# Gate/up- and down-projection of a decoder layer as 2x2 block products with 7 multiplications

## Chip, cores and metric

The kernel runs on one core of one Trainium2 chip, in one launch. The metric is the time of the run on the device in microseconds (us), as the median of several runs; lower is better. All inputs lie in HBM, and the result is written to HBM.

## What is computed

One pre-norm decoder layer over 512 tokens and a model width of 2048, in float32. Three token mixers (the functions are left out here) give `mix`; it is projected and added to the residual, a second RMSNorm feeds a gated MLP with a causal convolution of width 3 over the tokens, and a last RMSNorm closes.

```python
D_MODEL, SEQ, D_FF, CONV_W = 2048, 512, 5632, 3

def rms_norm(x, g):
    x32 = x.astype(jnp.float32)
    y = x32 * lax.rsqrt(jnp.mean(x32 * x32, axis=-1, keepdims=True) + EPS)
    return (y * g.astype(jnp.float32)).astype(x.dtype)

def conv_glu_ffn(h, w_up, conv_w, conv_b, w_down):
    a = h @ w_up
    a = lax.conv_general_dilated(a, conv_w[:, None, :], window_strides=(1,),
                                 padding=[(CONV_W - 1, 0)], ...) + conv_b
    gate, up = a[..., :D_FF], a[..., D_FF:]
    return (jax.nn.silu(gate) * up) @ w_down

x = x + mix @ w_out[l]
h = rms_norm(x, norm_ffn[l])
x = x + conv_glu_ffn(h, w_up[l], conv_w[l], conv_b[l], w_down[l])
return rms_norm(x, norm_final)
```

## The kernel before

Everything is held transposed: model or hidden columns lie on the 128 partitions, the 512 tokens along the free axis. A weight block of 128 x 128 is the stationary operand of a matmul, an activation tile of 128 x 512 the moving one. Each float32 operand X is split in two, `hi` (ScalarE's copy to fp32r, line 81 for weights) and `lo` = X - `hi` (VectorE, line 82), and each block product is three matmuls into one PSUM bank: hi by hi, hi by lo, lo by hi (`step`, lines 95 to 97; `accumulate` runs it over the inner blocks). `split` (lines 106 and 107) does the same for activations.

Weights come in pieces of up to `WS` = 1024 columns, 8 blocks: `stage` (lines 74 to 83) loads one on SyncE's DMA queue into one of two `raw` buffers and splits it into one of four `hi` and one of four `lo` buffers, at high priority, so that loads and splits stand as early in each engine's row as the buffers allow. `tiles_of` cuts a weight row into two such pieces. The Tile framework sets the order of each engine's instructions and the waits between them.

The mixers fill the first 674 us. Then come:

- The out-projection (674 to 849 us): 16 rows `d` of 16 blocks. `resid(d, ps)` loads the residual `x` on GpSimd's queue (line 747), adds the result (748), scales and splits it into the normalization's numerator `hh` and `hl` (754, 755), squares it on ScalarE (761) and sums the squares on GpSimd into `sacc` (762). All 16 tiles of the new residual, `x2`, stay in SBUF.
- The FFN (from 849 us): `FG` = 4 groups of `FT` = 11 hidden tiles. `up(f)` is two units, gate and up, of 16 blocks and 48 matmuls of 512 columns each. The first call also forms the row scale `rs2` from `sacc`. `conv` (lines 783 to 786) scales each result by `rs2` out of PSUM, and adds the three taps on ScalarE and VectorE; then come SiLU, the gating product (798) and the split into `hidh`, `hidl`, which stay in SBUF. After 11 of these, the down-projection of the group: for each of 16 rows `d`, 11 blocks, 33 matmuls, and one VectorE addition onto `x2[d]`.
- The last group's down-projection: the first 7 blocks of each row as before; the last `NL` = 4 blocks in two halves of 256 tokens (`last`, lines 841 to 843, addition in 845). `finish(0)`, the final norm of the first half with its output, stands inside the second half; `finish(1)` (lines 860 to 871) ends the kernel: the row scale `r3s` and one scaling for each row, partly on VectorE (870).

## Time and profile before

| | |
|---|---|
| Time, median of 3 runs (lowest to highest) | 2304.11 us (2303.01 to 2304.51) |
| Span of the profiled execution (its own time) | 2303.2 us |
| TensorE busy | 2275.0 us, 99% |
| VectorE busy | 1217.3 us, 53% |
| ScalarE busy | 878.4 us, 38% |
| GpSimd busy | 87.0 us, 4% |
| DMA, mean over the span | 98 GB/s |

The profile is of one execution, and its own time is the span; that is 0.9 us under the median of the runs. PE is TensorE's matmul row, PEld its weight loads, which lie beside matmuls, DVE is VectorE, ACT ScalarE, POOL GpSimd and SP SyncE. A matmul's recorded duration is longer than its share of the engine, since matmuls overlap; how much of TensorE one takes is read from the distance between the starts of two. Busy time of an engine says how much it had to do, not whether anything waited for it; the chain that ended last and the idle time in front of instructions say that.

### The profile page before, as it was taken

How to read it: one execution, taken by the hardware profiler on the slowest of the kernel's cores; microseconds unless marked ns; L12 is line 12 of the kernel's file. 1: busy time of each engine (PE TensorE's matmuls, PEld its weight loads, DVE VectorE, ACT ScalarE, POOL GpSimd, SP SyncE). 2: the span in 40 equal slices, each digit the busy share in tenths (PEclk: the TensorE clock that was granted, in tenths of full speed). 3: DMA queues.
4: the chain of work that ended last, by engine and by line, in shares of the span. 5: the costliest groups of instructions: out<-in, count | busy, mean ns of one | idle time of the engine just before them, and what ended most of it. 6: DMA issues, size and time to landing. Idle time of an engine off the chain costs nothing.

```text
span 2303.2 us, 27199 instructions
## 1 busy us (share of the span) xinstructions
PE 2275.0 (99%) x10788; PEld 1917.5 (83%) x10788; DVE 1217.3 (53%) x1991; ACT 878.4 (38%) x1272; POOL 87.0 (4%) x150
## 2 busy tenths in 40 slices
PE   8999999999999999999999999999999999999998
PEld 7988889888888888888888888888888888888887
DVE  7689576667675335444334444334544433454446
ACT  6536566755564223333223333222333222333223
POOL 4010000000011110000000000000000000000001
PEclk9999999999999999999999999999999999999999
DMA  5333322222233322232333322333233233323233
GB/s 180 103 96 123 100 78 74 74 71 83 89 118 121 101 93 99 92 100 84 95 105 101 101 94 91 91 99 111 92 100 96 84 95 110 101 94 99 71 113 110
DMA packets 72816, 226.49 MB, mean 98 GB/s; under 512 B 9220, under 2 KB 11674, under 8 KB 72688
## 3 DMA queue, kind: packets, MB, share of 16 engines
q1 hardware_dynamic: 67824, 211.40, 28.9%
q0 software_dynamic: 4720, 13.35, 1.7%
q8 instruction: 84, 1.38, 0.3%
q14 instruction: 44, 0.36, 0.1%
q10 hardware_dynamic: 144, 0.01, 0.0%
HBM read 220.50 MB, written 6.18 MB: 98 GB/s over the span
## 4 chain that ended last, share of the span: by engine, by line
PE 94%; DVE 2%; ACT 2%; DMA 1%; issue 1%; POOL 0%; DVEq 0%; ACTq 0%; POOLq 0%
PE pj L95 24%; PE pj L96 24%; PE pj L97 24%; PE mx L95 3%; PE mx L97 3%; PE mx L96 3%; PE pmv L205 1%; PE pmv L207 1%; PE pmv L206 1%; PE pa L440 1%; ACT hi L81 1%; DMA x<-in_xT_dram 1%; PE psc L284 0%; PE ptr L638 0%; DVE lo L82 0%
## 5 line engine op out<-in xcount | busy, mean ns | idle before, releaser
L81 ACT ACTIVATE hi<-raw 128x1024 fp32r<-128x1024 f32 (+5 forms) x438 | 420.3, 960 | 996.5 <-PE pj L96 764.3
L82 DVE TENSOR_TENSOR lo<-raw,hi 128x1024 fp32r<-128x1024 f32 (+5 forms) x438 | 483.7, 1105 | 461.1 <-ACT hi L81 460.7
L95 PE MATMUL pj<-hh,hi 128*128 128x512 f32 x1408 | 547.8, 389 | 0.0
L97 PE MATMUL pj<-hh,lo 128*128 128x512 f32 x1408 | 547.8, 389 | 0.0
L96 PE MATMUL pj<-hh,hi 128*128 128x512 f32 x1320 | 513.5, 389 | 0.0
L95 PEld LDWEIGHTS pj<-hh,hi 128*128 128x128 f32 x1408 | 264.4, 188 | 54.9
L97 PEld LDWEIGHTS pj<-hh,lo 128*128 128x128 f32 x1408 | 264.4, 188 | 54.7
L96 PEld LDWEIGHTS pj<-hh,hi 128*128 128x128 f32 x1320 | 247.9, 188 | 51.3
L95 PE MATMUL pj<-xh,hi 128*128 128x512 f32 (+1 forms) x608 | 232.2, 382 | 0.9 <-ACT ia L250 0.9
L96 PE MATMUL pj<-xl,hi 128*128 128x512 f32 (+1 forms) x608 | 231.7, 381 | 0.0
L97 PE MATMUL pj<-xh,lo 128*128 128x512 f32 (+1 forms) x608 | 231.0, 380 | 0.0
L783 DVE TENSOR_TENSOR a<-pj,rs 128x512 f32<-128x512 f32 x88 | 60.8, 691 | 291.4 <-PE pj L97 289.4
L95 PEld LDWEIGHTS pj<-xh,hi 128*128 128x128 f32 x608 | 114.2, 188 | 19.2 <-ACT ia L250 1.1
L97 PEld LDWEIGHTS pj<-xh,lo 128*128 128x128 f32 x608 | 114.2, 188 | 18.0
L96 PEld LDWEIGHTS pj<-xl,hi 128*128 128x128 f32 x608 | 114.3, 188 | 17.8
L95 PE MATMUL pj<-hidh,hi 128*128 128x512 f32 x320 | 124.5, 389 | 0.0
L96 PE MATMUL pj<-hidl,hi 128*128 128x512 f32 x320 | 124.5, 389 | 0.0
L97 PE MATMUL pj<-hidh,lo 128*128 128x512 f32 x320 | 124.5, 389 | 0.0
L95 PE MATMUL mx<-hidh,hi 128*128 128x512 f32 x320 | 124.5, 389 | 0.0
L96 PE MATMUL mx<-hidl,hi 128*128 128x512 f32 x320 | 124.5, 389 | 0.0
L97 PE MATMUL mx<-hidh,lo 128*128 128x512 f32 x320 | 124.5, 389 | 0.0
L97 PE MATMUL pj<-mh,lo 128*128 128x512 f32 x256 | 99.9, 390 | 0.0
(339 smaller groups left out, 3014.0 us busy)
## 6 DMA issues: line engine op xcount, KB each, us to landing
raw<-in_wu_dram SPq DMA_DIRECT2D x176, 512.0 KB, 3.6
raw<-in_wst_dram SPq DMA_DIRECT2D x76, 512.0 KB, 3.6
raw<-in_wd_dram SPq DMA_DIRECT2D x48, 384.0 KB, 3.1
raw<-in_wo_dram SPq DMA_DIRECT2D x32, 512.0 KB, 3.6
raw<-in_wd_dram SPq DMA_DIRECT2D x48, 320.0 KB, 2.9
x<-in_xT_dram POOLq DMA_DIRECT2D x32, 256.0 KB, 5.7
raw<-in_wcv_dram SPq DMA_DIRECT2D x8, 512.0 KB, 3.7
raw<-in_wai_dram SPq DMA_DIRECT2D x8, 512.0 KB, 3.8
```

The lines of the kernel that those rows point to most:

```text
L81: ACT.activation(hi[:, :cols], raw[:, :cols], AF.Copy)
L82: DVE.tensor_tensor(lo[:, :cols], raw[:, :cols], hi[:, :cols], op=ALU.subtract)
L95: PE.matmul(ps, wh, ah[:, lo:], start=first, stop=False)
L96: PE.matmul(ps, wh, al[:, lo:], start=False, stop=False)
L97: PE.matmul(ps, wl, ah[:, lo:], start=False, stop=last)
L205: PE.matmul(ps[t], ah[:, ts], wh, start=(k == 0), stop=False)
L206: PE.matmul(ps[t], al[:, ts], wh, start=False, stop=False)
L207: PE.matmul(ps[t], ah[:, ts], wl, start=False, stop=(k == KT - 1))
L440: PE.matmul(pa[:, c * 192:(c + 1) * 192], x[:, cc * P:(cc + 1) * P], y[:, cc * 192:(cc + 1) * 192], start=(c == 0), stop=(c == 1), skip_gr ...
L783: DVE.tensor_tensor(a, ps, rs2, op=ALU.mult)
```

## The change

The gate/up-projection and the down-projection no longer multiply block by block. Each takes 2x2 blocks at a time: A11, A12, A21, A22 of the weights and B11 to B22 of the activations, by a Winograd form of Strassen's scheme, with 7 products for 8. A block is a set of 128 x 128 weight blocks against 256 tokens. The rows of blocks are two tiles of output columns (for the up-projection the gate and the up tile of the same `f`; for the down-projection two neighbouring rows), the columns of blocks the even and the odd inner tiles, and the halves of B the first and the last 256 tokens. The seven products use the weights A11, S1 = A21 + A22, S2 = S1 + A11, A12, S3 = A21 + A11, S4 = S2 + A12 and A22, in this order; the minus signs of the scheme lie on the activations.

- `blocks_of` (lines 827 to 850) makes the weights of one pair. SyncE's queue loads one block twice into the two halves of a new tile `s13` (827, 1 MB for 8 inner blocks), and a DMA from GpSimd's queue adds two other blocks onto it as it writes (829, `accum_op=ALU.add`), so that S1 and S3 stand there. A11, A12 and A22 are loaded plainly into `raw` buffers (833). VectorE forms S2 (845) and S4 (848) from them, and all seven are split (838 and 839). There are two `s13` buffers, two for S2 and S4 together, four `raw`, three `hi` and three `lo`.
- `pair` (from 869) runs the seven products, each h inner blocks of three matmuls with 256 columns. ScalarE copies three intermediate results out of PSUM (866), VectorE forms the four results from PSUM and those copies (878, 880, 882 and line 902, or ScalarE for the last one). In the up-projection the results land in a tile `a`, scaled by `rs2` before the taps.
- The activations are combined likewise: `combos_a` and `combos_b` (with `halves_of`, lines 748 and 750) build the tiles for the seven products out of two pairs of tiles, ahead of each projection.
- All 44 up pairs run first; their results go to HBM as `hidd` (909). The down-projection then runs in `GROUPS` of 12, 12, 12 and 8 hidden tiles: it loads the group's tiles back as `hd` (934), combines them into 44 `td` buffers, and runs 8 pairs of rows. The new residual is kept in HBM as `x2d` too; the results of the first three groups are added onto it by an accumulating DMA (948). In the last group it is read back and added on VectorE, and the final norm runs over all 512 tokens at once; `last` and `finish` are gone.
- The weights are laid out in blocks in `_layout`, outside the launch. The SBUF pools are allocated from two sides, and a new pool's tiles wait for the old tiles that lay in their place.

```diff
-FG = 4
-FT = NF // FG
...
+GROUPS = [12, 12, 12, 8]
...
+    x2d = dram.tile([KT // 2, P, 2, T], F32, name="x2d")
+    hidd = dram.tile([NF // 2, P, 2, T], F32, name="hidd")
...
+    def halves_of(src, sgn, alloc):
+        h, l = alloc(), alloc()
+        n = src.shape[1]
+        h, l = [v.rearrange("p (k t) -> p k t", t=H)[:, :n] for v in (h, l)]
+        ACT.activation(h, src, AF.Copy, scale=float(sgn))
+        if sgn > 0:
+            DVE.tensor_tensor(l, src, h, op=ALU.subtract)
+        else:
+            DVE.scalar_tensor_tensor(l, src, -1.0, h, op0=ALU.mult, op1=ALU.subtract)
+        return h, l
...
+    def combos_a(b1, b2, alloc):
+        b11, b12, b22 = b1[:, :, :H], b1[:, :, H:], b2[:, :, H:]
+        r = {"a11": halves_of(b11, 1, alloc)}
+        DVE.tensor_tensor(b11, b12, b11, op=ALU.subtract)
+        r["s1"] = halves_of(b11, -1, alloc)
+        DVE.tensor_tensor(b12, b22, b12, op=ALU.subtract)
+        DVE.tensor_tensor(b11, b22, b11, op=ALU.subtract)
+        r["s2"] = halves_of(b11, -1, alloc)
+        return r
...
+    def combos_b(key, b1, b2, alloc):
+        b11, b12, b21, b22 = b1[:, :, :H], b1[:, :, H:], b2[:, :, :H], b2[:, :, H:]
+        if key == "a22":
+            DVE.tensor_tensor(b11, b11, b21, op=ALU.subtract)
+        return halves_of({"a12": b21, "s3": b12, "s4": b22, "a22": b11}[key], 1, alloc)
...
+    hbs, early = [], []
...
     def resid(d, ps):
-        x = keep("x2")
+        x = stg.tile([P, T], F32, tag="x", bufs=3, name="x2")
         POOL.dma_start(x, xT[d])
         DVE.tensor_tensor(x, x, ps, op=ALU.add)
...
-        ACT.activation(h, x, AF.Copy, scale=g)
-        DVE.scalar_tensor_tensor(l, x, g, h, op0=ALU.mult, op1=ALU.subtract)
...
+        nc.sync.dma_start(x2d[d // 2][:, d % 2, :], x)
+        if d % 4 == 0:
+            hbs.append([hb.tile([P, 2, T], F32, tag="hb", bufs=8, name="hb") for e in range(2)])
+        ACT.activation(hbs[d // 4][d % 2][:, (d % 4) // 2, :], x, AF.Copy, scale=cst[:, C_NFFN + d:C_NFFN + d + 1])
...
+        if d % 4 == 3:
+            early.append(combos_a(*hbs[d // 4], lambda: hp.tile([P, T], F32R, tag="h", bufs=24, name="tc")))
...
+    for key in LATE:
+        for c, (b1, b2) in zip(early, hbs):
+            c[key] = combos_b(key, b1, b2, lambda: slot("tc"))
+    s_st.close()
+    s_hb.close()
+    s_wp.close()
...
+    def blocks_of(src, n):
+        with tc.high_priority():
+            s13 = wide("s13", 2, n, "s13", m=2)
+            nc.sync.dma_start(s13.rearrange("p (e c) -> p e c", e=2),
+                              bass.AP(tensor=src.tensor, offset=src.offset, ap=[[4 * n, P], [0, 2], [1, n]]))
+            POOL.dma_start(s13, src[:, n:3 * n], accum_op=ALU.add)
+            r = {"s1": s13[:, :n], "s3": s13[:, n:]}
+            for i, key in ((2, "a11"), (3, "a12"), (1, "a22")):
+                r[key] = wide("raw", 4, n, key)
+                nc.sync.dma_start(r[key], src[:, i * n:(i + 1) * n])
+            out = {}
...
+            def hl(key):
+                hi, lo = wide("hi", 3, n, "hi", F32R), wide("lo", 3, n, "lo", F32R)
+                ACT.activation(hi, r[key], AF.Copy)
+                DVE.tensor_tensor(lo, r[key], hi, op=ALU.subtract)
+                out[key] = hi, lo
...
+            hl("a11")
+            hl("s1")
+            r["s2"] = wide("s24", 2, n, "s2")
+            DVE.tensor_tensor(r["s2"], r["s1"], r["a11"], op=ALU.add)
+            hl("s2")
+            r["s4"] = wide("s24", 2, n, "s4")
+            DVE.tensor_tensor(r["s4"], r["s2"], r["a12"], op=ALU.add)
+            hl("a12")
+            hl("s3")
+            hl("s4")
+            hl("a22")
+        return out
...
+    def product(ps, w, key, tcs, h, first):
+        hi, lo = w[key]
+        for k in range(h):
+            wh, wl = hi[:, k * P:(k + 1) * P], lo[:, k * P:(k + 1) * P]
+            th, tl = [v[:, k % 2, :] for v in tcs[k // 2][key]]
+            PE.matmul(ps, wh, th, start=first and k == 0, stop=False, skip_group_check=True)
+            PE.matmul(ps, wh, tl, start=False, stop=False, skip_group_check=True)
+            PE.matmul(ps, wl, th, start=False, stop=(k == h - 1), skip_group_check=True)
...
+    def pair(w, tcs, h, c11, c12, c22, c21):
+        a, b, c = pj([P, H], "pa"), mx([P, H], "pb"), mx([P, H], "pc")
+        product(a, w, "a11", tcs, h, True)
+        p1 = part(a, "p1")
+        product(c, w, "s1", tcs, h, True)
+        p5 = part(c, "p5")
+        product(a, w, "s2", tcs, h, False)
+        u2 = part(a, "u2")
+        product(b, w, "a12", tcs, h, True)
+        DVE.tensor_tensor(c11, b, p1, op=ALU.add)
+        product(a, w, "s3", tcs, h, False)
+        DVE.scalar_tensor_tensor(c22, a, -1.0, p5, op0=ALU.mult, op1=ALU.subtract)
+        product(c, w, "s4", tcs, h, False)
+        DVE.tensor_tensor(c12, c, u2, op=ALU.add)
+        product(a, w, "a22", tcs, h, False)
+        c21(a)
...
-        a, y = ft("a"), ft("y")
-        DVE.tensor_tensor(a, ps, rs2, op=ALU.mult)
+        y = cv.tile([P, T], F32, tag="y", bufs=4, name="y")
...
-    def up(f):
-        pss = [pj(), pj()]
-        for s in range(2):
-            accumulate([pss[s]], [tiles_of(wu[2 * f + s])], h2)
+    for f in range(NF):
+        w = blocks_of(wu[f], WS)
+        av = cv.tile([P, 2, T], F32, tag="a", bufs=2, name="a")
...
+        pair(w, early, KT // 2, ag[:, :H], ag[:, H:], au[:, H:], late.append)
...
+        DVE.scalar_tensor_tensor(au[:, :H], late[0], -1.0, rs2[:, :H], op0=ALU.mult, op1=ALU.mult)
+        DVE.tensor_tensor(au[:, H:], au[:, H:], rs2[:, H:], op=ALU.mult)
+        DVE.tensor_tensor(ag, ag, rs2, op=ALU.mult)
...
-        h, l = slot("hidh"), slot("hidl")
-        split(yg, h, l)
-        return h, l
...
-    for gidx in range(FG):
-        hid = [up(gidx * FT + i) for i in range(FT)]
...
-        for d in range(KT):
-            w = tiles_of(wd[gidx * KT + d], FT)
-            ps = mx() if d % 2 else pj()
-            accumulate([ps], [w], hid)
-            DVE.tensor_tensor(x2[d], x2[d], ps, op=ALU.add)
...
+        nc.sync.dma_start(hidd[(f // 4) * 2 + f % 2][:, (f % 4) // 2, :], yg)
...
+    for g, size in enumerate(GROUPS):
+        h = size // 2
...
+        alloc = lambda: td.tile([P, T], F32R, tag="t", bufs=44 if g < len(GROUPS) - 1 else 28, name="td")
...
+                v = hd.tile([P, 2, T], F32, tag="hd", bufs=6 if g < len(GROUPS) - 1 else 4, name="hd")
+                nc.sync.dma_start(v, hidd[(g0 // 4 + s) * 2 + e])
...
+        for b1, b2 in hts:
+            tcs.append(combos_a(b1, b2, alloc))
+        for key in LATE:
+            for c, (b1, b2) in zip(tcs, hts):
+                c[key] = combos_b(key, b1, b2, alloc)
+        for m in range(KT // 2):
+            w = blocks_of(wd[g][m], h * P)
+            cs = cv.tile([P, 2, T], F32, tag="a", bufs=2, name="cs")
+            pair(w, tcs, h, cs[:, 0, :H], cs[:, 0, H:], cs[:, 1, H:],
+                 lambda a: ACT.activation(cs[:, 1, :H], a, AF.Copy, scale=-1.0))
+            if g < len(GROUPS) - 1:
+                POOL.dma_start(x2d[m], cs, accum_op=ALU.add)
+                continue
...
+            nc.sync.dma_start(x, x2d[m])
+            DVE.tensor_tensor(x, x, cs, op=ALU.add)
...
+    r3 = spread(rstd_cols([sf, sums[0], sums[1]], D))
...
-    def last(half):
-        hs = slice(half * HT, (half + 1) * HT)
...
-        for d in range(KT):
-            if half and d == 4:
-                finish(0)
-            ps = (mx if d % 2 else pj)([P, HT])
-            for i in range(NL):
-                ks = slice(i * P, (i + 1) * P)
-                hh, hl = hid[FT - NL + i]
-                PE.matmul(ps, wl_hi[:, d, ks], hh[:, hs], start=(i == 0), stop=False)
-                PE.matmul(ps, wl_hi[:, d, ks], hl[:, hs], start=False, stop=False)
-                PE.matmul(ps, wl_lo[:, d, ks], hh[:, hs], start=False, stop=(i == NL - 1))
...
-    def finish(half):
-        hs = slice(half * HT, (half + 1) * HT)
-        r3 = spread(rstd_cols(sums[half], D, 2), 2)
...
-    sums = {}
-    last(0)
-    last(1)
-    finish(1)
+                DVE.scalar_tensor_tensor(o[:, e], x, gain, r3, op0=ALU.mult, op1=ALU.mult)
+        nc.sync.dma_start(outT[m], o)
...
+    wu = np.concatenate([up[1, 0], up[1, 1], up[0, 0], up[0, 1]], axis=2)
```

**VectorE in the up-projection, before**, somewhat behind the first third of it. `raw` and `lo` are weight pieces, `a` and `y` the convolution's tiles, `pj` a result in PSUM.

```order
L82 TENSOR_TENSOR lo<-raw,hi 128x1024 [waits DMAHW1_49,Activation_49]
L785 SCALAR_TENSOR_TENSOR y<-a,cst,y 128x511 [waits Activation_49]
L786 SCALAR_TENSOR_TENSOR y<-a,cst,y 128x510 [waits DVE_49]
L82 TENSOR_TENSOR lo<-raw,hi 128x1024 [waits DMAHW2_49,PE_49,Activation_49]
L783 TENSOR_TENSOR a<-pj,rs_7416 128x512 [waits PE_49]
L82 TENSOR_TENSOR lo<-raw,hi 128x1024 [waits DMAHW3_49,Activation_49]
L785 SCALAR_TENSOR_TENSOR y<-a,cst,y 128x511 [waits Activation_49]
L786 SCALAR_TENSOR_TENSOR y<-a,cst,y 128x510 [waits DVE_49]
L798 TENSOR_TENSOR y<-y 128x512 [waits DVE_49]
L107 TENSOR_TENSOR hidl<-y,hidh 128x512 [waits Activation_49]
```

**VectorE there, after.** The weight tiles are of two pairs, f+1 and f+2. `s_9445` and `s_9681` are `s13` of f+1 and f+2, `s_9462` and `s_9468` S2 and S4 of f+1, `s_9698` and `s_9704` those of f+2, `a_9450` is A12 of f+1, `a_9684` and `a_9686` are A11 and A12 of f+2. A wait on DMASW is one for a DMA of GpSimd's queue, here the accumulating one.

```order
L839 TENSOR_TENSOR lo<-s_9462,hi 128x1024 [waits Activation_49]
L890 SCALAR_TENSOR_TENSOR y<-a,cst,y 128x511 [waits DMAHW5_49,Activation_49]
L845 TENSOR_TENSOR s_9698<-s_9681,a_9684 128x1024 [waits DMAHW3_49,DMAHW4_49,DMASW6_49,DVE_49]
L839 TENSOR_TENSOR lo<-a_9450,hi 128x1024 [waits PE_49,Activation_49]
L891 SCALAR_TENSOR_TENSOR y<-a,cst,y 128x510 [waits DVE_49]
L908 TENSOR_TENSOR y<-y 128x512 [waits DVE_49]
L839 TENSOR_TENSOR lo<-s_9445,hi 128x1024 [waits PE_49,Activation_49]
L839 TENSOR_TENSOR lo<-s_9468,hi 128x1024 [waits PE_49,Activation_49]
L848 TENSOR_TENSOR s_9704<-s_9698,a_9686 128x1024 [waits DMAHW5_49,DVE_49]
L878 TENSOR_TENSOR a<-pb,p_9514 128x256 [waits PE_49]
```

Between the splits of pair f+1 there now stand the two sums of pair f+2, and the first of them (line 845) waits for the accumulating DMA of pair f+2; the splits of A12, S3 and S4 of pair f+1 stand behind it.

**SyncE's queue from the out-projection on, before.** `in_wo`, `in_wu` and `in_wd` are the weights of the out-, the up- and the down-projection.

```order
L78 DMA raw<-in_wst_dram 128x1024 x4
L78 DMA raw<-in_wo_dram 128x1024 x32
L78 DMA raw<-in_wu_dram 128x1024 x44
L78 DMA raw<-in_wd_dram 128x768
L78 DMA raw<-in_wd_dram 128x640
```

**SyncE's queue in the up-projection, after**, one pair's rows.

```order
L909 DMA hidd<-y 128x512
L827 DMA s_8501<-in_wu_dram 128x2x1024
L833 DMA a_8504<-in_wu_dram 128x1024
L833 DMA a_8506<-in_wu_dram 128x1024
L833 DMA a_8508<-in_wu_dram 128x1024
```

The queue carried weight loads alone; now the doubled load of each pair stands in a row with its three plain ones and with the store of the pair before last's result.

**VectorE at the end of the out-projection, before.** `x_7406` is a residual tile, `hh` and `hl` its split.

```order
L748 TENSOR_TENSOR x_7406<-x_7406,pj 128x512 [waits DMASW4_49,PE_49]
L82 TENSOR_TENSOR lo<-raw,hi 128x1024 [waits DMAHW3_49,Activation_49]
L755 SCALAR_TENSOR_TENSOR hl<-x_7406,cst,hh 128x512 [waits Activation_49]
L82 TENSOR_TENSOR lo<-raw,hi 128x1024 [waits DMAHW4_49,PE_49,Activation_49]
L82 TENSOR_TENSOR lo<-raw,hi 128x1024 [waits DMAHW5_49,PE_49,Activation_49]
L82 TENSOR_TENSOR lo<-raw,hi 128x1024 [waits DMAHW6_49,PE_49,Activation_49]
L131 TENSOR_SCALAR rv<-pcol 128x4 [waits PE_49]
```

**VectorE there, after.** `tc` and `hb` are combined activations, `s_7539`, `s_7556` and `s_7562` are S1 and S3, S2 and S4 of the first up pair, `a_7542` and `a_7544` its A11 and A12, `s_7793`, `s_7810` and `a_7796` tiles of the second.

```order
L748 TENSOR_TENSOR tc<-hb,tc 128x512 [waits Activation_49]
L766 TENSOR_TENSOR hb<-hb 128x2x256 [waits DVE_49]
L748 TENSOR_TENSOR tc<-hb,tc 128x512 [waits Activation_49] x10
L845 TENSOR_TENSOR s_7556<-s_7539,a_7542 128x1024 [waits DMAHW2_49,DMAHW0_49,DMASW5_49]
L839 TENSOR_TENSOR lo<-a_7542,hi 128x1024 [waits Activation_49]
L839 TENSOR_TENSOR lo<-s_7539,hi 128x1024 [waits Activation_49]
L839 TENSOR_TENSOR lo<-s_7556,hi 128x1024 [waits Activation_49]
L848 TENSOR_TENSOR s_7562<-s_7556,a_7544 128x1024 [waits DMAHW3_49]
L845 TENSOR_TENSOR s_7810<-s_7793,a_7796 128x1024 [waits DMAHW1_49,DMAHW5_49,DMASW6_49,DVE_49]
L839 TENSOR_TENSOR lo<-a_7544,hi 128x1024 [waits PE_49,Activation_49]
```

Splits of the first up weights stood among those of the last residual tiles; now they stand behind all combinations, and the sum that waits for the first accumulating DMA stands ahead of the first split.

## Rows read from the trace of the kernel before

**Rows 1.** The page: span, busy time by engine, TensorE's clock in 40 slices

```profile
span 2303.2 us, 27199 instructions
...
PE 2275.0 (99%) x10788; PEld 1917.5 (83%) x10788; DVE 1217.3 (53%) x1991; ACT 878.4 (38%) x1272; POOL 87.0 (4%) x150
...
PEclk9999999999999999999999999999999999999999
```

**Rows 2.** The page: the chain that ended last, by engine

```profile
PE 94%; DVE 2%; ACT 2%; DMA 1%; issue 1%; POOL 0%; DVEq 0%; ACTq 0%; POOLq 0%
```

**Rows 3.** FFN: us, busy PE, PEld, DVE, ACT, POOL, clock, DMA share, GB/s

```profile
849.00:2290.40 1441.40, 1441.33 (x6552) 1201.87 (x6550) 642.22 (x808) 428.07 (x535) 4.83 (x6) 1.00 0.31 96
```

**Rows 4.** Timeline (start, duration), TensorE, up-projection: first and last of ten

```profile
1239.76 0.39 PE L97 MATMUL pj<-hh,lo 128*128 128x512 f32 x1
...
1241.80 0.39 PE L97 MATMUL pj<-hh,lo 128*128 128x512 f32 x1
```

**Rows 5.** Timeline, TensorE, last halves: first and last of 66 matmuls

```profile
2255.09 0.28 PE L843 MATMUL pj<-hidh,wl_lo 128*128 128x256 f32 x1
...
2262.89 0.28 PE L842 MATMUL mx<-hidl,wl_hi 128*128 128x256 f32 x1
```

**Rows 6.** Waits: instruction, what released it: total us, count, longest us

```profile
ACT hi L81 <- PE pj L96: 764.3, 292, 4.8
```

**Rows 7.** Timeline, VectorE, up-projection: a split and the next instruction, in brackets idle

```profile
1221.33 1.23 DVE L82 TENSOR_TENSOR lo<-raw,hi 128x1024 fp32r<-128x1024 f32 x1 [0.17 <-ACT hi L81]
1222.47 0.74 DVE L785 SCALAR_TENSOR_TENSOR y<-a,cst,y 128x511 f32<-128x511 f32 x1
```

**Rows 8.** Groups by line and shape: count | busy us, mean ns | idle before

```profile
L82 DVE TENSOR_TENSOR lo<-raw,hi 128x1024 fp32r<-128x1024 f32 x300 | 367.5, 1225 | 289.5 <-ACT hi L81 289.3
L81 ACT ACTIVATE hi<-raw 128x1024 fp32r<-128x1024 f32 x300 | 317.8, 1060 | 663.1 <-PE pj L96 585.1 <-PE pmv L206 29.2 <-PE mx L96 16.1
...
L786 DVE SCALAR_TENSOR_TENSOR y<-a,cst,y 128x510 f32<-128x510 f32 x88 | 66.0, 750 | 3.1
...
L798 DVE TENSOR_TENSOR y<-y 128x512 f32<-128x512 f32 x44 | 30.5, 693 | 1.6
...
L762 POOL TENSOR_TENSOR sacc<-sacc,sq 128x512 f32<-128x512 f32 x15 | 25.5, 1700 | 136.1 <-ACT sq L761 136.0
...
L754 ACT ACTIVATE hh<-x,cst 128x512 fp32r<-128x512 f32 x16 | 11.4, 710 | 3.0 <-DVE x L748 3.0
...
L761 ACT ACTIVATE sq<-x 128x512 f32<-128x512 f32 x15 | 9.2, 616 | 0.0
...
L747 POOL DMA_DIRECT2D x<-in_xT_dram x16 | 8.5, 538 | 0.9 <-ACT pth L106 0.5 <-issue 0.2
...
L845 DVE TENSOR_TENSOR x<-x,pj 128x256 f32<-128x256 f32 x16 | 6.7, 417 | 2.6 <-PE pj L843 2.5
```

**Rows 9.** DMA issues: count, KB each, median us from issue to landing

```profile
raw<-in_wu_dram SPq DMA_DIRECT2D x176, 512.0 KB, 3.6
...
raw<-in_wd_dram SPq DMA_DIRECT2D x16, 192.0 KB, 2.4
...
brep<-bline POOLq DMA_DIRECT2D x1, 1920.0 KB, 19.8
```

**Rows 10.** Timeline, TensorE behind its idle time near the start

```profile
23.39 0.48 PE L207 MATMUL pia<-lo,xh 128*128 128x336 f32 x1
23.67 0.48 PE L205 MATMUL pia<-hi,xh 128*128 128x336 f32 x1
...
26.57 0.32 PE L205 MATMUL pia<-hi,xh 128*128 128x336 f32 x1
26.73 0.31 PE L206 MATMUL pia<-hi,xl 128*128 128x336 f32 x1
```

**Rows 11.** Timeline, VectorE: the last half's final scalings

```profile
2294.53 4.40 DVE L870 SCALAR_TENSOR_TENSOR og<-x,cst,pspr 128x256 f32<-128x256 f32 x11 [1.20 <-ACT r3s L860]
```

**Rows 12.** DMA issues between 187 and 215 us, while `brep` runs

```profile
raw<-in_wst_dram SPq DMA_DIRECT2D x5, 512.0 KB, 6.6
```

## What the change does to the time

> **What bounds the kernel now.** I read the page's busy times first: TensorE is busy for 2275.0 of 2303.2 us at the full granted clock, VectorE for 53%, ScalarE for 38% [rows 1]. The chain that ended last says the same, 94% of it TensorE [rows 2]. Then I cut the span into stages. The feed-forward part (FFN) runs from 849.0 to 2290.4 us, 1441.4 us, with TensorE never idle, VectorE at 45% and the DMA engines at 31% for 96 GB/s [rows 3]. Its 512-column matmuls start 2.04/9 = 0.2267 us apart [rows 4], the 256-column ones of its last 48 us 7.80/65 = 0.1200 us [rows 5]. 6,144 x 0.2267 + 384 x 0.1200 = 1438.9 us: the stage is its matmuls and 2.5 us. ScalarE waits for TensorE to give weight buffers back, 292 times and 764 us in all [rows 6]; nothing waits for a weight load. So only fewer TensorE microseconds help here, and only while the other engines keep up.
>
> **TensorE's share.** An up pair (128 gate and 128 up columns) was 96 matmuls of 512 columns, 96 x 0.2267 = 21.76 us. It becomes 7 products x 8 x 3 = 168 of 256 columns, 168 x 0.1200 = 20.16 us. So 7 for 8 gives 7.4%, not 12.5%, since two half-width matmuls take 0.240 us for 0.2267. A down pair takes 126 x 0.1200 = 15.12 us in the groups of 12 and 84 x 0.1200 = 10.08 us in the group of 8. In all 7,392 + 3,024 + 672 = 11,088 matmuls, 1330.6 us, 108 us less than 1438.9. This is the whole gain.
>
> The Trainium skill (TensorE: Matmul & The Clock Gate, section Back-to-back issue gap) gives N/2.4 + 2.5 ns, 109 ns for 256 columns, where the trace has 120. By it the 11,088 matmuls would take 1211 us, 120 us less again. The row decides, since it has the same type, shape and order of operands.
>
> **VectorE, ScalarE and DMA, in the steady state.** VectorE's work for an up pair: 7 lo halves and 2 weight sums of 1,024 columns, which follow each other by 1.14 us [rows 7] although one takes 1.23 [rows 8], 10.3 us; five 256-column operations on results at some 0.35 (0.417 alone [rows 8]), 1.8; one 512-column scaling 0.6, four convolution taps at 0.75 [rows 8], 3.0, and the gating product 0.6: 16.3 of 20.16 us. ScalarE: 7 x 1.06 and some 3.5 us more, 11. Both fit beside TensorE. DMA: 1 MB into the sum tile, 1 MB accumulated onto it, 1.5 MB of plain blocks and 0.25 MB of result are 195 GB/s, 63% by 96 GB/s at a 31% share [rows 3]. The sums fit; what may not fit is a chain.
>
> **The chain through the sum buffers.** `s13` has two buffers. In the program order of VectorE the sum S2 of pair f+2, which waits for the accumulating DMA, stands ahead of the lo half of A12 of pair f+1, and the lo half of S3 of pair f+1, which frees the next `s13`, stands behind that. So one round per pair is: load 1 MB, GpSimd issue, accumulate 1 MB (call it A), S2 sum, lo A12, tap, gating product, lo S3. The load: 512 KB land in 3.6 us and 192 KB in 2.4 [rows 9], 3.84 us per 1,024 KB and 1.7 fixed, so 5.5 us. Issue 0.54 (the `x` loads [rows 8] in kind), VectorE 1.14 + 1.14 + 0.78 + 0.69 + 1.23 = 5.0, three handovers of 0.17 [rows 7] 0.5. The round is 11.5 + A, hidden while A is under 8.6 us. The trace has no accumulating DMA. Bounds: as a plain 1 MB, 5.5 us; at the pace of the dearest row, `brep` (DRAM to DRAM from GpSimd, 1,920 KB in 19.8 us [rows 9]), 10.6. Below a plain load it can't be, since it moves the same bytes from HBM. I take the middle, 8.0: it reads one side more than a plain load, but one side lies in SBUF. Then the round is 19.5 us, hidden. Behind VectorE's wait stand the lo halves of A12, S3 and S4, and TensorE waits for them.
>
> The same round for 768 KB is 8.3 + 6.25 (4.6 to 7.9) = 14.6 us against 15.12, hidden; for 512 KB 6.5 + 4.4 (3.6 to 5.3) = 10.9 against 10.08, 0.8 short in 8 pairs. FFN without its joints: 44 x 20.16 + 24 x 15.12 + 8 x 10.9 + 2.5 = 1339.6, **102 us less** than 1441.4.
>
> **The joints, which cost nothing before.**
> Out-projection to up: the first `s13` load waits for the last row of the residual: add 0.69 (as the gating product), gain 0.71, square 0.62 and GpSimd's sum 1.70 [rows 8], 3.7 us after the last matmul. Then load 5.5, issue 0.54, A 8.0, S2 sum 1.14 (it stands ahead of the first lo half), lo 1.23 and handovers 0.5: TensorE idles 20.6 us (18 to 24). It starts again at half clock, as after its idle time at 21 us: 336-column matmuls come every 0.28 us until 26 us and every 0.16 behind that [rows 10], some 2.2 us lost. Together 23.
> Up to down: activations must be combined on VectorE, 11 operations of 512 columns for each set of four k-tiles, 33 for a group of 12, at 0.6 us 20 us. Their tiles lie where tiles that the last up pair reads lie, so they come free from its A12 product on, and they queue with that pair's convolution and with the next lo halves. From 8.6 us ahead of the joint VectorE has some 37 us to do until the A22 product of the first down pair, which TensorE reaches 21.6 us later if nothing stops it: 16 us.
> Group to group, twice: 44 buffers for 42 tiles, so most waits for the S2 product of the old group's last pair; 31 us of VectorE against 21.6: 10 us each.
> Into the last group: its loads wait for the old group's last products; 5.5 us for the first MB, then 22 combining operations (13 us) and 5 us of lo halves against 8.6 us: 15 us.
> Tail: the 11 final scalings took 4.4 us at 256 columns [rows 11] and go to 512, one output DMA doubles, and no half is finished early: 5 us.
> Sum 23 + 16 + 20 + 15 + 5 = **79 us** (50 to 95). The out-projection itself gains VectorE work and 16 stores of 256 KB, and is covered by its 10.9 us of TensorE per row.
>
> **Forecast.** 2303.2 - 101.8 + 79 = 2280.4 us of span; the median of the runs is 0.9 us above the span (2304.11), so **2281 us**, own range 2262 to 2299.
>
> **Rivals.**
> *The accumulate is bound by its two reads* (slower than before): A = 1.7 + 2 x 3.84 = 9.4. The up round is then 20.9, 0.7 over, 44 times: 33 us; the 768 KB round 15.8, 0.7 over, 24 times: 16; the 512 KB one 12.0, 1.1 over, 8 times: 9; the start 1.4. That is 2281 + 59 = 2340 us. For it: both reads would share an engine's time. Against: single 512 KB loads moved 3.84 us per MB with most of the DMA time free, so the second read may overlap. It decides from A = 9.0 us, where the excess of 68 pairs has eaten the gain of 23 us. The Trainium skill (Collectives: The Full Stack, section The bandwidth ceiling: the fold count and why AG ≠ RS ≠ AR) states that an add in a DMA takes two source reads on one ring and about halves the rate (62.28 to 32.35 GB/s); by its rule this rival is what happens. No row shows it.
> *The kernel's own loads slow it too*: a 512 KB load took 6.6 us beside `brep` [rows 12], not 3.6. With `brep`'s pace and 1.1 us more, the up round is 23.2, 3.0 over; with 1.9 over in the 768 KB pairs and 1.5 in the 512 KB ones: 2281 + 134 + 45 + 12 + 4 = 2476 us.
> *The joints are half covered*, because ScalarE and VectorE catch up while TensorE waits: 49 us in place of 79, 2251 us.
> *Shorter spacing* (109 ns): the rounds then hold the pairs at 19.5 and 14.6 us, 2281 - 29 - 12 = 2240 us. The Trainium skill's rule cited above would give it; the rows speak against it [rows 5].
> That the change doesn't do what it says can't be: the product counts stand in the program.
>
> **How the numbers follow.** Forecast 0.37, joints half covered 0.13, shorter spacing 0.02, two reads 0.30 (2299 to 2390, with 0.07 of it inside 0.2% of before), own loads 0.18 (from 2390). The time is the forecast's, 2281. The range 2240 to 2400 leaves out some 0.02 below and 0.17 above. About 0.2% is what a measurement of this kernel can tell: faster 0.37 + 0.13 + 0.02 = 0.52, same 0.07, slower 0.23 + 0.18 = 0.41. It is close to even, because the gain of 108 us and the cost of the joints differ by less than the doubt on A.
>
> **What would show it.** In the trace after: 256-column matmuls 0.120 us apart inside a product; up pairs 20.2 us apart if the round is hidden, else as far apart as 11.5 + A, with VectorE's S2 sum waiting for the accumulating DMA and TensorE for the lo half; the accumulating DMA's own time to landing, 8 us by the forecast, 9.4 by the first rival; gaps of TensorE of 23, 16, 10, 10 and 15 us at the joints, with half clock behind the first. The forecast falls if A is over 9 us or if VectorE's order makes TensorE wait in every pair.

## The result and the profile after

The changed kernel took **2518.68 us** (median of 4 runs, 2513.85 to 2530.32), the kernel before 2303.78: ratio 1.0939, 95% interval 1.0911 to 1.0967. The forecast was 2281 us and its range ended at 2400.

The page of the changed kernel answers to [rows 1]: span, busy time by engine, TensorE's busy tenths and granted clock in 40 slices.

```profile
span 2521.4 us, 38495 instructions
...
PE 2279.5 (90%) x15356; PEld 2121.7 (84%) x15356; DVE 1699.3 (67%) x2621; ACT 1184.5 (47%) x1790; POOL 169.0 (7%) x245
...
PE   8999999999999679899899899889997998989785
...
PEclk9999999999999889999999999999998998989897
```

TensorE now has holes all through the FFN, and its granted clock falls a little there (0.951 over the span; 0.96 in the up pairs below). The timeline of one up pair shows the hole and its cause, by engine: start, duration, in brackets the idle time ahead. L827 is the load of `s13`, L829 the accumulating DMA, L845 the sum S2, L839 a lo half, L862 the matmul with a lo half.

```profile
1211.09 0.38 SPq L827 DMA_DIRECT2D s<-in_wu_dram  x1
...
1218.91 0.88 POOL L829 DMA_DIRECT2D s<-in_wu_dram  x1 [21.43 <-DVE a L904]
...
1229.70 1.23 DVE L845 TENSOR_TENSOR s<-s,a 128x1024 f32<-128x1024 f32 x1 [6.62 <-issue]
1230.85 1.22 DVE L839 TENSOR_TENSOR lo<-a,hi 128x1024 fp32r<-128x1024 f32 x1
1231.98 0.74 DVE L891 SCALAR_TENSOR_TENSOR y<-a,cst,y 128x510 f32<-128x510 f32 x1
1232.76 0.69 DVE L908 TENSOR_TENSOR y<-y 128x512 f32<-128x512 f32 x1
1233.37 2.35 DVE L839 TENSOR_TENSOR lo<-s,hi 128x1024 fp32r<-128x1024 f32 x2
...
1234.62 0.38 SPq L827 DMA_DIRECT2D s<-in_wu_dram  x1
```

```profile
1228.72 0.28 PE L861 MATMUL pb<-tc,hi 128*128 128x256 f32 x1
1232.12 0.58 PE L862 MATMUL pb<-tc,lo 128*128 128x256 f32 x1 [3.12 <-DVE lo L839]
```

The two loads of `s13` lie 23.5 us apart, and the round between them can be followed: load 1211.09 to 1218.91, 7.8 us; issue and accumulate until VectorE starts S2 at 1229.70, 10.8; S2, lo of A12, tap, gating product and the first lo of S3 until the next load, 4.9. VectorE waited 6.62 us for the accumulate with the lo half of A12 queued behind, and TensorE 3.12 us for that half. ("issue" names no releaser; in the order of the program the wait is for the accumulating DMA.) Next come 40 up pairs, from the fourth A12 product to the last, by windows (us, busy by engine, clock, DMA share, GB/s), against [rows 3]:

```profile
972.30:1904.76 932.46, 849.97 (x6722) 841.69 (x6721) 661.21 (x803) 411.22 (x520) 34.90 (x40) 0.96 0.64 169
```

932.46 / 40 = **23.3 us a pair**, where TensorE needs 20.16. The transfers themselves, as in [rows 9] (count, KB each, median us from issue to landing):

```profile
a<-in_wu_dram SPq DMA_DIRECT2D x132, 512.0 KB, 4.8
s<-in_wu_dram SPq DMA_DIRECT2D x44, 1024.0 KB, 7.5
s<-in_wu_dram POOLq DMA_DIRECT2D x44, 1024.0 KB, 10.4
```

Both transfers of the round are longer than the prediction had them (5.5 and 8.0).

### The profile page after: what moved, and what is told of

Read it like the earlier page. It is cut to its first block, busy times and chain, and to the rows that moved or that the text cites. A ratio compares the mean times of both kernels' runs of the same rounds, so it can differ in the third digit from the quotient of the medians.

```text
span 2521.4 us, 38495 instructions
## 1 busy us (share of the span) xinstructions
PE 2279.5 (90%) x15356; PEld 2121.7 (84%) x15356; DVE 1699.3 (67%) x2621; ACT 1184.5 (47%) x1790; POOL 169.0 (7%) x245
## 5 line engine op out<-in xcount | busy, mean ns | idle before, releaser
L838 ACT ACTIVATE hi<-s 128x1024 fp32r<-128x1024 f32 (+2 forms) x304 | 287.8, 947 | 389.4 <-PE pc L861 212.0
L838 ACT ACTIVATE hi<-a 128x1024 fp32r<-128x1024 f32 (+2 forms) x228 | 216.0, 947 | 459.9 <-PE pb L861 252.6
L860 PE MATMUL pa<-tc,hi 128*128 128x256 f32 x1408 | 399.3, 284 | 24.8 <-ACT hi L838 24.8
L862 PE MATMUL pa<-tc,lo 128*128 128x256 f32 x1408 | 398.5, 283 | 0.5 <-DVE lo L839 0.5
L861 PE MATMUL pa<-tc,hi 128*128 128x256 f32 x1408 | 398.9, 283 | 0.0
L839 DVE TENSOR_TENSOR lo<-s,hi 128x1024 fp32r<-128x1024 f32 (+2 forms) x304 | 323.8, 1081 | 56.6 <-ACT hi L838 55.9
L845 DVE TENSOR_TENSOR s<-s,a 128x1024 f32<-128x1024 f32 (+2 forms) x76 | 82.5, 1085 | 364.1 <-issue 247.7
L860 PEld LDWEIGHTS pa<-tc,hi 128*128 128x128 f32 x1408 | 268.4, 191 | 25.3 <-ACT hi L838 25.3
L862 PEld LDWEIGHTS pa<-tc,lo 128*128 128x128 f32 x1408 | 266.9, 190 | 0.8 <-DVE lo L839 0.8
L861 PEld LDWEIGHTS pa<-tc,hi 128*128 128x128 f32 x1408 | 267.4, 190 | 0.0
L839 DVE TENSOR_TENSOR lo<-a,hi 128x1024 fp32r<-128x1024 f32 (+2 forms) x228 | 246.4, 1081 | 15.6 <-ACT hi L838 12.5
L861 PE MATMUL pa<-td,hi 128*128 128x256 f32 x704 | 206.2, 293 | 20.2 <-DVE td L748 19.8
L860 PE MATMUL pa<-td,hi 128*128 128x256 f32 x704 | 206.7, 294 | 14.8 <-ACT td L746 12.5
L860 PE MATMUL pc<-tc,hi 128*128 128x256 f32 x704 | 199.5, 283 | 7.1 <-ACT hi L838 7.1
L862 PE MATMUL pa<-td,lo 128*128 128x256 f32 x704 | 204.3, 290 | 0.1
L861 PE MATMUL pc<-tc,hi 128*128 128x256 f32 x704 | 199.4, 283 | 0.0
L862 PE MATMUL pc<-tc,lo 128*128 128x256 f32 x704 | 199.1, 283 | 0.0
## 6 DMA issues: line engine op xcount, KB each, us to landing
s<-in_wu_dram POOLq DMA_DIRECT2D x44, 1024.0 KB, 10.4
```

The costliest lines, as they stand in the source:

```text
L838: ACT.activation(hi, r[key], AF.Copy)
L839: DVE.tensor_tensor(lo, r[key], hi, op=ALU.subtract)
L845: DVE.tensor_tensor(r["s2"], r["s1"], r["a11"], op=ALU.add)
L860: PE.matmul(ps, wh, th, start=first and k == 0, stop=False, skip_group_check=True)
L861: PE.matmul(ps, wh, tl, start=False, stop=False, skip_group_check=True)
L862: PE.matmul(ps, wl, th, start=False, stop=(k == h - 1), skip_group_check=True)
```

## The experiments

### The order on VectorE

```diff
+            with tc.issue_after(s3_lo[-1]) if s3_lo else ExitStack():
                 DVE.tensor_tensor(r["s2"], r["s1"], r["a11"], op=ALU.add)
```

`s3_lo` holds the instruction that makes the lo half of S3 of the pair before.

> The sum S2 of the next pair is queued on VectorE behind the lo half of S3 of the pair before it; nothing else is changed. Round theory: the changed kernel's pair takes 23.4 us because load of s13, accumulate and five VectorE instructions form one round through VectorE's row (7.8 + 10.8 + 4.9 in the pair at 1211 us). With the new order the lo half that frees s13 no longer waits for the accumulate, so the round is 7.8 + 10.8 = 18.6 us against TensorE's 20.16 and is hidden: up pairs 20.2 to 21 us, down pairs of 12 near 15.2, TensorE's wait ahead of A12 gone; time 2518.7 less 44 x 2.8, 20 x 1.2 and 8 x 1.5, about 2360 us (2340 to 2400). Rival, throughput: GpSimd's accumulating queue and the other loads can't bring more than one pair in 23 us whatever the order; then the wait only moves behind A12, and the time stays above 2480 us.

Measured: **2327.4 us**, 1.0103 of the kernel before (1.0086 to 1.0120). The same 40 pairs, and a stretch of the down-projection:

```profile
967.08:1773.48 806.40, 806.40 (x6722) 806.40 (x6721) 671.60 (x801) 411.49 (x520) 34.90 (x40) 1.00 0.74 195
1829.27:1919.99 90.72, 90.72 (x759) 90.72 (x757) 59.78 (x77) 43.63 (x69) 10.48 (x12) 1.00 0.90 223
```

806.40 / 40 = 20.16 us, TensorE without a gap at full clock (the second line is six down pairs of 12 tiles, 15.12 us each), although the accumulate got no faster:

```profile
a<-in_wu_dram SPq DMA_DIRECT2D x132, 512.0 KB, 4.5
s<-in_wu_dram SPq DMA_DIRECT2D x44, 1024.0 KB, 7.0
s<-in_wu_dram POOLq DMA_DIRECT2D x44, 1024.0 KB, 10.8
```

This settles the cause. The DMA engines bring a pair in 20.16 us, more traffic per microsecond than before (195 against 169 GB/s). A slow accumulate cost time only because one VectorE instruction that waits for it stood ahead of the one that frees the next `s13`. Of the 197 us between the two spans, 131 lie in the up stage and 66 behind it. The throughput theory fell, and so did my number for the gain (158 us): I had counted 36 us for the down pairs and nothing for the joints between the stages, and the joints behind the up stage shrank too, by some 26 us.

### Why the accumulate takes 10.4 us

```diff
-            POOL.dma_start(s13, src[:, n:3 * n], accum_op=ALU.add)
+            POOL.dma_start(s13, src[:, n:3 * n])
```

> The DMA from GpSimd's queue writes its two blocks onto s13 instead of adding them (so S1 and S3 are wrong: the sums are left out); bytes, queue, waits and order are the same. Two-reads theory: the adding is what makes it 10.4 us to landing, so it falls to the 7.5 us of the other 1 MB load, the up round from 23.4 to about 20.5 and the time to about 2518.7 - 44 x 2.9 - 24 x 1.3 - 8 x 1.8, some 2345 us. Own-loads theory: the DMA is slow because three plain loads and a store run beside it, adding or not; it stays at 10 us, the time above 2480 us. In between, each has its share: every microsecond of it is 44 us in the up stage.

Measured: 2341.35 us, ratio 1.0168 (1.0150 to 1.0186). The same bytes from the same queue land in 7.2 us when nothing is added, as fast as the other 1 MB load:

```profile
a<-in_wu_dram SPq DMA_DIRECT2D x132, 512.0 KB, 4.8
s<-in_wu_dram SPq DMA_DIRECT2D x44, 1024.0 KB, 7.4
s<-in_wu_dram POOLq DMA_DIRECT2D x44, 1024.0 KB, 7.2
```

The adding costs 3.2 us, or 3.6 against the run with the later S2 (10.8), whose up pairs come every 20.16 us as nearly all do here. The Trainium skill (Collectives: The Full Stack, section The bandwidth ceiling: the fold count and why AG ≠ RS ≠ AR) puts a reduce-scatter, whose add needs two source reads, at about half the rate of an all-gather, measured on rings between cores. Here the trace shows a factor of 1.44 to landing (1.50 at the same pace of the pairs), so the direction holds, and the size doesn't carry over to this DMA.

The next run takes the up pairs' own plain loads away:

```diff
             for i, key in ((2, "a11"), (3, "a12"), (1, "a22")):
+                if n == WS and key in kept:
+                    r[key] = kept[key]
+                    continue
                 r[key] = wide("raw", 4, n, key)
                 nc.sync.dma_start(r[key], src[:, i * n:(i + 1) * n])
+                if n == WS:
+                    kept[key] = r[key]
```

> In the up stage A11, A12 and A22 are loaded for the first pair only and kept (so all later pairs use the first pair's blocks there); s13's load, the accumulate and the store stay. Own-loads theory: beside no plain loads the s13 load lands in 5.5 us (median 7.5 now) and the accumulate in about 8 (10.4), the up round falls from 23.4 to 11.5 + 8 = 19.5, hidden behind 20.16: time about 2518.7 - 44 x 3.2 = 2378 us (2370 to 2400). Two-reads theory: the s13 load falls to 5.5 but the accumulate stays at 10, so the round is 21.5: about 2435 us.

Measured: 2390.95 us, ratio 1.0380 (1.0357 to 1.0402). From the second on, the up pairs come every 20.16 us again; the down-projection was left as it is in the changed kernel.

```profile
s<-in_wu_dram SPq DMA_DIRECT2D x44, 1024.0 KB, 6.0
s<-in_wu_dram POOLq DMA_DIRECT2D x44, 1024.0 KB, 8.1
```

Without the pair's own plain loads the `s13` load is 1.5 us shorter and the accumulate 2.3. So both theories had a share: 3.2 us of adding, 2.3 of the kernel's own loads, and either one taken away hides the round behind the pair (in the run before, 7 of the 43 distances between pairs were still 20.4 to 22.2 us). The accumulate of 8.0 us that I had taken is the one of a stage without plain loads.

### The sums on VectorE

```diff
-            POOL.dma_start(s13, src[:, n:3 * n], accum_op=ALU.add)
...
             hl("a11")
+            DVE.tensor_tensor(r["s1"], r["s1"], r["a22"], op=ALU.add)
             hl("s1")
...
+            DVE.tensor_tensor(r["s3"], r["s3"], r["a11"], op=ALU.add)
             hl("s3")
```

> No accumulating DMA: s13 is loaded as before, and VectorE adds A22 and A11 onto its halves (two more instructions of 1.14 us per up pair). Round theory: the round without 10.8 us of accumulate is far under 20.16, so TensorE sets the pair again unless VectorE does, whose work is 16.3 + 2.3 = 18.6 us of 20.16: 20.2 to 21.5 us per up pair, 15.1 to 15.6 per down pair, 2518.7 - 44 x 2.6 - 24 x 1.2 - 8 x 1.5, about 2365 us (2340 to 2420). If VectorE's row instead makes TensorE wait in every pair (a round of its own), the pair stays over 22 us and the time over 2440 us.

The loads of A12 and A22 also change places, since A22 is now needed first.

Measured: 2392.46 us, ratio 1.0383 (1.0367 to 1.0398); up pairs mostly 21.3 us. The forecast of the time held, but not because VectorE is full: it is busy 86% of the up stage, 18.4 us a pair. The waits (what waited for what: us in all, times, longest) name a new one, in nearly every up pair:

```profile
PE pa L861 <- ACT p L867: 37.9, 42, 1.3
```

TensorE's product S2 waits until ScalarE has copied the result of A11 out of PSUM; at 1193 us that copy stood in ScalarE's row behind a convolution tap, which waited 0.96 us for VectorE. Without the accumulate the pair still is 1.2 us over, so the reordered DMA version is the better one.

### The stages ahead of the FFN

In the changed kernel the out-projection ended at 859.4 us, not at 849.0. Its 512-column matmuls were 0.2333 us apart instead of 0.2267. Stores and combinations had been added to that stage; for the matmuls themselves, what had changed was where the weight tiles lie. Addresses stand in no trace: those given below follow from the order and the sizes of the tiles in the programs.

```diff
-    res = ctx.enter_context(tc.tile_pool(name="res", bufs=1))
-    wp = ctx.enter_context(tc.tile_pool(name="wp", bufs=1))
+    wp = ctx.enter_context(tc.tile_pool(name="wp", bufs=1, side="right"))
+    res = ctx.enter_context(tc.tile_pool(name="res", bufs=1, side="right"))
```

> The kernel before, with one part of the change alone: the pools of the weights and of the residual are allocated from the right end of SBUF, where the weight tiles' addresses leave 32 when divided by 64 (0 before). The traces behind the change show the out-projection's 512-column matmuls 0.2333 us apart, where they were 0.2267. Address theory: all 512-column matmuls take 6.7 ns more, 6,144 of the FFN 41 us and the stages ahead 10: about 2355 us. Rival: the slower matmuls come from the change's other traffic in that stage (stores, combinations); then this kernel stays at 2304 us.

Measured: 2357.28 us, ratio 1.0231 (1.0214 to 1.0248): the kernel before, slowed by 53 us by this alone. Then the same with 32 bytes free at the right end (`pad.tile([P, 8], F32)` ahead of `wp`):

> As the run with the pools on the right, with 32 bytes left free at the right end, so that all addresses are multiples of 64 again. If the remainder of the address is what costs 6.7 ns a matmul: 2304 us, as the kernel before. If it is the right end itself (the distance from the activations): as the run without the gap, some 2355 us.

Measured: 2355.13 us, ratio 1.0215 (1.0200 to 1.0230). The theory of a multiple of 64 fell. The next two separate the end of SBUF from the distance between the operands: 160 bytes on the right (`[P, 40]`), and 128 bytes between the activations and everything behind them on the left (`[P, 32]`).

> As the run with 32 bytes left free at the right end (2355 us), with 160 bytes: the weight tiles then stand at the same remainder of 2,048 as in the kernel before (1,856), and as the activations. If a matmul is 6.7 ns slower because its weights and its activations lie at different places within such a stretch, this kernel is back at 2304 us. If it is the right end of SBUF as such, it stays at 2355 us.

> The kernel before with 128 bytes left free between the activations and all that lies behind them; all pools stay on the left. If the place within a stretch of 2,048 bytes counts (weights 1,984, first activations 1,856), it slows to about 2355 us, or somewhere between where both operands moved; if it is the right end, it stays at 2304 us.

Measured: 160 bytes on the right 2304.36 us, ratio 1.0001 (0.9991 to 1.0010), no loss at all; the shift on the left 2329.98 us, ratio 1.0113 (1.0098 to 1.0128). So the right end is harmless, and it is the place of the weights relative to the activations that counts. The timelines of TensorE show the first and the 31st of a row of matmuls: weights on the right; the same with 160 bytes; then the shift on the left, in the out-projection and in the down-projection, where only the weights moved.

```profile
780.06 0.39 PE L97 MATMUL pj<-mh,lo 128*128 128x512 f32 x1
...
787.06 0.39 PE L97 MATMUL pj<-mh,lo 128*128 128x512 f32 x1
```

```profile
780.15 0.39 PE L100 MATMUL pj<-mh,lo 128*128 128x512 f32 x1
...
786.95 0.39 PE L100 MATMUL pj<-mh,lo 128*128 128x512 f32 x1
```

```profile
779.90 0.39 PE L99 MATMUL pj<-mh,lo 128*128 128x512 f32 x1
...
786.86 0.39 PE L99 MATMUL pj<-mh,lo 128*128 128x512 f32 x1
...
1130.63 0.39 PE L97 MATMUL pj<-hidh,hi 128*128 128x512 f32 x1
...
1137.63 0.39 PE L97 MATMUL pj<-hidh,hi 128*128 128x512 f32 x1
```

30 matmuls take 7.00, 6.80, 6.96 and 7.00 us. In the up-projection of the shifted kernel, 15 of the 16 activation tiles moved together with the weights (`hp` lies behind the gap), and one stayed (`slot`; its `lo` half is the `hl` below):

```profile
1006.79 0.39 PE L99 MATMUL pj<-hh,lo 128*128 128x512 f32 x1
...
1011.55 0.39 PE L99 MATMUL pj<-hh,lo 128*128 128x512 f32 x1
1011.78 0.40 PE L97 MATMUL pj<-hh,hi 128*128 128x512 f32 x1
1012.01 0.39 PE L98 MATMUL pj<-hl,hi 128*128 128x512 f32 x1
...
1012.94 0.39 PE L99 MATMUL pj<-hh,lo 128*128 128x512 f32 x1
```

The first 21 matmuls take 4.76 us, 0.680 for three, as in the kernel before; the six around the tile that stayed take 1.39, 0.695 for three. Within one kernel, only matmuls whose operands moved apart, and the few beside them, are slow.

### The first joint, and a version that gains

The first `s13` load of the changed kernel went out only when the last activation had been combined, 13 us behind the last out-projection matmul (timeline of SyncE; the load is the first of the two):

```profile
872.61 0.93 SPq L827 DMA_DIRECT2D s<-in_wu_dram  x2
```

`s13` lay where the combined residual `hb` lay. The next kernel is the one with the later S2 and 32 bytes, with the weight pools in another order:

```diff
-    ww = region(ctx, "ww", "right")
+    ww = {"raw": region(ctx, "wraw", "right"), "s24": region(ctx, "ws24", "right"),
+          "s13": region(ctx, "ws13", "right")}
+    ww["hi"] = ww["lo"] = region(ctx, "whl", "right")
```

> The kernel with S2 queued later (2327 us), plus the 32 bytes, plus another order of the weight pools at the right end: s13 and the raw blocks now lie where the out-projection's weights lay, not where the combined residual lies, so the first s13 load no longer waits for the last combination (it was issued at 872.8 us, 13 us behind the last out-projection matmul). Theory of the joint: the load goes out with the last weights, some 13 us earlier, S1 is ready when the combinations end, and TensorE starts 10 us earlier and doesn't stop behind A11 (7 us): the 38 us of this joint fall to about 21; the 10 us ahead of it go with the addresses: 2327 - 17 - 10 = 2300 us (2292 to 2312). Rival: the joint is set by the combinations on VectorE and ScalarE alone; then it falls by 7 us at most, 2310 us.

Measured: 2300.26 us, ratio 0.9985 (0.9975 to 0.9994). The total was as forecast, the way to it only in part. The load went out at once, and the joint fell from 38 us to 24, where 21 had been forecast: TensorE still waited 20.3 us (857.8 to 878.1), since the high-priority sums S2 and S4 of the first pair now stood among the combinations and held them up. Of the 10 us ahead of the FFN all but 1.6 stayed, as the runs on the place explain. In their stead the up pairs gave 10 us, 19.94 us each in place of 20.16: three 256-column matmuls took 0.356 us instead of 0.360. That was not forecast, so the total was luck by that much.

The next keeps that up-projection and puts back the plain down-projection, with 512-column matmuls over the blocks in four groups of 11:

```diff
+    def hidden(f, pool):
+        v = hd.tile([P, T], F32, tag="hd", bufs=3, name="hd")
+        POOL.dma_start(v, hidd[f])
+        h, l = [pool.tile([P, T], F32R, tag="t", bufs=2 * FT, name="hid") for e in range(2)]
+        split(v, h, l)
+        return h, l
...
+        for d in range(KT):
+            w = row(wd[g * KT + d], FT)
+            ps = mx() if d % 2 else pj()
+            accumulate([ps], [w], hid)
+            if d < FT:
+                nxt.append(hidden((g + 1) * FT + d, ta if g % 2 else tb))
+            cs = csp.tile([P, T], F32, tag="cs", bufs=10, name="cs")
+            ACT.activation(cs, ps, AF.Copy)
+            POOL.dma_start(x2d[d], cs, accum_op=ALU.add)
```

> As the run before it in the up-projection, but the down-projection is that of the kernel before: 512-column matmuls over the blocks, 4 groups of 11, here with the hidden tiles read back from HBM and split into two sets of 22 buffers, so that a group's tiles are ready before the group starts. Term theory: the down-projection's seven products gained 16 x 44 x 3 x 0.2267 = 479 less 443 us = 35 and cost 69 us at its four joints and 14 at the tail, so leaving them out is worth about 45 us: 2303.2 - 70.4 (44 pairs x 1.6) + 21 (first joint) + 5 (up to down) = 2259 us (2250 to 2285), faster than the kernel before. If up to down costs as much as with the combinations (23 us), 2280 us.

Measured: 2278.57 us, ratio 0.9889 (0.9875 to 0.9904). 22 us better than with seven products in the down-projection, where 45 had been expected: 30 matmuls cost 6.97 us there as well (the place again, 11 us), the first joint stayed at 24 us where 21 had been counted, and behind the last of the 256-column matmuls the tail took 19.6 us, where the kernel before has 12.9. Of this the trace shows 1.05 us as a wait for an output tile, not the 4 of the next expectation; the rest of it was not taken apart. Up to down cost nothing. The next one changes these three: 160 bytes, S2 of the first pair behind the combinations and the first `lo` half, four more output tiles.

> The kernel with 7 products in the up-projection alone (2278.6 us), with 160 bytes in place of 32, the first sum S2 queued behind the last combination of activations and behind the first lo half (in its trace S2 stood ahead of three combinations and held them 3.7 us), and four more output tiles in the tail (an output tile was waited for 4 us). Order and tail: 2278.6 - 5 - 4 = 2270 us. If the place of the weights is what slows matmuls, another 10 us ahead of the FFN and 14 in the down-projection: 2246 us.

Measured: 2261.41 us, ratio 0.9816 (0.9801 to 0.9830). It came between the two numbers: the 512-column matmuls were back at 0.680 us for three and the first joint fell to 19 us, but the 256-column matmuls of the up-projection went back to 0.360, which gave 10 us away again. In the last kernel each stage has the place that suits it: the weights of the up- and down-projection and the down-projection's activations stand 128 bytes further.

> The kernel of 2261.4 us with one thing changed, where tiles stand: the weight tiles of the up- and down-projection and the down-projection's activations stand 128 bytes further, so that in the up-projection weights and activations differ by 128 bytes modulo 2,048 and in the out- and down-projection they still agree. Place theory, from the traces of the kernels with 32 and with 160 bytes left free: three 256-column matmuls take 0.356 us at this difference and 0.360 without, three 512-column ones 0.680 without: 7,392 / 3 x 0.004 = 10 us less, 2251.5 us, the up pair 19.94 us. If the 0.356 came from something else in those kernels, 2261 us.

Measured: **2255.28 us**, ratio 0.9794 (0.9778 to 0.9811), 6 of the 10 us; 40 up pairs lie in some 797 us again, with TensorE busy throughout:

```profile
945.00:1742.00 797.00, 797.00 (x6719) 797.00 (x6718) 668.15 (x800) 412.18 (x522) 35.67 (x42) 1.00 0.72 195
```

The other 4 us are at the first joint, where TensorE waited 4.72 us for the `hi` half of S1 (1.04 in the run before): the first `s13` load, which waits for out-projection matmuls in both, went out at 848.2 us, where it had gone at 840.1. This is the fastest kernel of the study.

## Why the prediction was wrong, by its own steps

- **TensorE's share** held. A pair without waits takes exactly 20.16 us, one of 12 tiles 15.12 (windows of the run with the later S2), and the engine still has 108 us less to do.
- **VectorE, ScalarE and DMA fit**, as it said: in that run VectorE is busy for 671.6 / 40 = 16.8 us a pair (16.3 forecast), and the traffic is the 195 GB/s that were worked out.
- **The chain through the sum buffers is the step that failed, by two of its terms.** The structure was right, down to VectorE's 5.0 us (4.9 measured) and to TensorE's wait for the lo half of A12. The load was put at 5.5 us and takes 7.5 in the median, the accumulate at 8.0 and takes 10.4. So the round is 23.3 us and not 19.5, it exceeds the pair instead of fitting, and 40 pairs pay 3.1 us each. The same holds in the down pairs of 12 (mostly 16 to 18 us where 15.12 were forecast) and of 8 (12 to 17 where 10.9 were). Of the 238 us over the forecast, 191 went when one instruction was moved; of the 46 that stayed, 36 are the joints and 10.5 the stages ahead of the FFN, both below.
- **Where these terms came from** is the lesson of it. The load was fitted from [rows 9], medians of a stage with the DMA engines at 31%; the prediction itself worked out 63% for the new stage and then priced the round's transfers as if they ran alone. The run without the pair's plain loads shows both transfers nearly as it had them, 6.0 and 8.1 us; the plain loads beside them add 1.5 and 2.3, and this is what the sum lacked. [rows 12] showed what company does (6.6 us for 3.6), and the rival built on it gave 23.2 us a pair and 2476 us; it had 0.18. The price of the add was not far off: the forecast put 2.5 us on it over a plain load of 5.5, and it costs 3.2 in full traffic (8.1 against 6.0, so 2.1, beside no plain loads).
- **The joints** were 79 us in the forecast. In the run with the later S2 they can be read one by one against 20.16, 15.12 and 10.08 us: out-projection to up 38 (23 forecast: the first load waited for the combinations, not only for the last residual row, 9 us, and from its issue to S2 it took 18.5 us where 14.0 stood), up to down 23 (16; between the two windows shown above lie 55.8 us, for which TensorE needs 33.1), group to group 10 and 10 (20 together), into the last group 19 (15), its pairs 7 too long (6), tail 14 (5: the squares of the last rows, a wait of 2.3 us, twice the scalings, and output tiles that VectorE waited 5.5 us for). They are 121 in all where 79 + 6 stood, so even with the rounds hidden the change loses: 2327 us.
- **The stages ahead of the FFN** were taken as unchanged. They cost 10.5 us, and the kernel before loses the same there when its pools alone are moved (its up-projection then starts at 859.4 us, too). The prediction treated the addresses of tiles as free.
- The bounds for the accumulate (5.5 to 10.6 us) held for its median of 10.4. The middle was a choice and no reading of a row; that it came so near the 8.1 us of a stage without plain loads is luck.

A third `s13` buffer, which might also hide the round, was not tried: counted by the tiles of the program, SBUF is full to 160 bytes, which no run shows. Over 40 pairs TensorE sat idle for 82.5 us and was busy for 43.6 us more than in the run with the later S2, at a granted clock of 0.96 in place of 1.00. The round shown above takes 23.5 us without a TensorE instruction in it, so in that pair the slower matmuls lay within the round and did not add to it; for the other pairs this is not shown.

## What to carry to other kernels

Price a transfer in the traffic of the stage that it will stand in, not in that of the stage whose trace shows it, and do so for every transfer of a round: here the load and the accumulate both slowed, by 1.5 and 2.3 us. An instruction that waits for a long transfer belongs in its engine's row behind everything that frees the buffers for the next one: here moving one sum was worth 191 us with the transfer as slow as ever. When seven products replace eight, count the joints too; here the seven products of the down-projection saved 35 us of matmuls, less than their joints cost, and the plain one was 22 us faster.

## What the runs showed of the hardware

The distance between a matmul's two operands in SBUF, worked out from the tiles of the programs, is worth up to 3% of a matmul. Three 512-column fp32r matmuls take 0.680 us when weights and activations stand at the same place modulo 2,048 bytes, also where both had moved by 128 bytes, and 0.695 to 0.700 when they are 128 or 160 bytes apart. For the kernel before, this is 51 to 53 us, more than most of the terms that the prediction weighed.

Three 256-column ones take 0.360 us at the same place or 160 bytes apart. At 128 bytes they took 0.356 in four kernels, but not always. In the kernel of 2300.26 us the first down group took 0.360 and the next 0.356, though the tiles of both lie 128 bytes apart modulo 2,048 (each pair of lines is a first and a 31st matmul):

```profile
1850.05 0.28 PE L869 MATMUL pb<-td,hi 128*128 128x256 f32 x1
...
1853.65 0.28 PE L869 MATMUL pc<-td,hi 128*128 128x256 f32 x1
...
1950.45 0.28 PE L869 MATMUL pa<-td,hi 128*128 128x256 f32 x1
...
1954.01 0.28 PE L869 MATMUL pa<-td,hi 128*128 128x256 f32 x1
```

So the place modulo 2,048 is not the whole condition for them. The runs don't tell what else counts, which power of two it is for the 512-column ones, nor why the two widths want opposite things.

An accumulating 1 MB DMA from HBM onto SBUF took 1.44 times as long to land as the same DMA without the add (10.4 against 7.2 us), and the three plain loads of the pair beside it lengthened it from 8.1 to 10.4.
